# Encoder trunk on one core: up-projection loads that alternate between two buffer tags, and the last plain pair reordered

## The chip, the cores and the metric

One core of a Trainium2 chip runs the whole program. The time is the device time of one execution in microseconds (us), as the median of the runs shown. All data is float32; each matmul operand is held as a high and a low part, and three matmuls (high x high, high x low, low x high) make one product step.

## The reference

Two layers on x of 1024 rows x 1024 columns. Layer 0 has a gated spatial mixer, layer 1 a banded attention; the change touches neither. Each is followed by the same feed-forward block (FFN), which is where the change lies:

```python
def sq_relu_mlp(h, w_up, w_down):
    return jnp.square(jax.nn.relu(h @ w_up)) @ w_down

h = h + rms_norm(m, g[1])
f = sq_relu_mlp(rms_norm(h, g[2]), w_up[layer], w_down[layer])
h = h + rms_norm(f, g[3])
```

`w_up` is 1024 x 4096 and `w_down` 4096 x 1024.

## The kernel before

**FFN up stage.** `ffn` (L380 on) computes relu(z w_up)^2, with z the normed stream. It goes through 16 pairs j of 128-column strips of `w_up`: strip j and strip j + 16. With z cut into four blocks (z11, z12, z21, z22: row halves by column halves) and a pair into b11, b21, b12, b22, a pair is a 2 x 2 block product. Pairs 0 to 2 are "plain": four results, each of two products (`plain`, L518). Pairs 3 to 15 use `blocks` (L555): seven products instead of eight, on sums of the blocks of z (s1, s2, s4, and a third sum that is written over z21 in place by `s3_in_place`, L514) and on differences of the weight blocks. A product is 12 matmuls of 128 x 512 (four steps of three). In `blocks` the products stand in this order on PE: b11 z11, t2 s2, b21 z12, t1 s1, t3 z21, t4 z22, b22 s4. The first and third add up in bank b1, the second and fifth in b2, the fourth and seventh in b3. The seventh may start only when DVE's L596 has read b3.

**Operands.** `load_pair` (L400) loads the two strips of a pair from HBM into two tiles of the tag "raw", which has two buffers. `Prep.step` 0 to 5 (L534) makes the operands out of them: each is a cast to the high part on ACT (L119) and a subtraction for the low part on DVE (L120); in between DVE forms the differences in place (L539, L542, L543, L548). Step 4 makes t3 and step 5 makes t4; after them the raw tiles are free. In `blocks` the steps of the *next* pair stand between the products of the running one, and SP's queue has the loads of pair j + 1 ahead of the spill of pair j - 1 (L464).

**Results.** ACT applies relu and square in place (`squared`, L447), POOL makes five sums of result blocks (`sums`, L452: place 0, then 5 and 6, then 2 and 3), and SP writes seven blocks per pair to `r_dram` (`spill`). `finish` (L610), called one block later, adds the seventh product (L611), squares it and makes sums 2 and 3.

**Order.** Inside the up stage all engines keep the order of the program text (`manual_schedule(engines=ALL)`), each engine in its own queue. The tag "row" has two buffers as well: during the up stage it holds the temporary sums of z, last the two parts of the third sum (`parts`, L512), which `s3_in_place` reads; afterwards `Post` (L290) takes one buffer for the norm weights (loaded by POOL's queue, L112) and one as scratch.

**Block 3 is special before the change** (`first`, L561): it holds the replacement of z21, steps 3 to 5 of its own pair, and, later than in the other blocks, the steps of pair 4:

```python
            nc.scalar.copy(left.t1, b1)
            if first:
                s3_in_place()
                prep.step(3)
                prep.step(4)
            else:
                before.finish()
                step(0)
```

**FFN down stage.** For each of seven products p (L727 on) eight steps jj load a block of `r_dram` (xr, L633) and one or two blocks of `w_down` (xw, L637), split them on ACT and DVE, and run 4 x 6 matmuls. The spill of pair 15 (`before.spill()`) stands at p = 0, jj = 1 of this loop; here a scheduler sets the order on each engine.

Of the kernel before, what the change touches and what calls it, by code (L numbers as in the profile page):

```python
# [18 lines left out]
NT = T // P  # L19
# [42 lines left out]
def trunk_kernel(ctx: ExitStack, tc: tile.TileContext, io: dict):  # L62
    nc = tc.nc
# [13 lines left out]
    ph = Pools(tc)  # L77
# [90 lines left out]
    def load_h(tag, t, h_src):  # L168
        h = ph.t(tag, f"h{t}")
        nc.sync.dma_start(h, h_src)  # L170
        return h
# [55 lines left out]
    def tick():  # L227
        if late:
            late.pop(0)()

    def out_mm(ps, src, units, t, ks):
        cs = slice(t * P, (t + 1) * P)
        for k in ks:
            uH, uL = units[k // 2]
            o = slice((k % 2) * 512, (k % 2) * 512 + 512)
            aH, aL = src(k, cs)
            mm3(ps, aH, aL, uH[:, o], uL[:, o], k == 0, k == NK - 1)
# [24 lines left out]
    def proj_second(src, zn, w, g_post, g_next, m_src, h_src, h_dst, htag, mtags, rest=None):  # L262


        def first(g, m, ps):
            nc.scalar.copy(m[:, 512:], ps[:, :512])
            if rest is not None:
                nc.vector.tensor_add(m[:, :512], ps[:, 512:], m[:, :512])

        tail = Tail(zn, g_post, g_next, h_dst, first)  # L270
        units = [load_unit(w[1, kp], f"wo1{kp}", W4[kp]) for kp in range(4)]
        if rest is not None:
            raw = ph.t("raw", "wo03r")
            nc.sync.dma_start(raw[:, :512], w[0, 3][:, 512:])
            split(rest[:, 0], rest[:, 1], raw[:, :512])
        for t in range(NT):
            ps = ph.t("big", f"po1{t}")
            m = ph.t(mtags[t % len(mtags)], f"m{t}")
            nc.sync.dma_start(m[:, :512], m_src[t])
            h = load_h(htag, t, h_src(t))  # L280
            out_mm(ps[:, :512], src, units, t, range(NK))
            if rest is not None:
                aH, aL = src(NK - 1, slice(t * P, (t + 1) * P))
                mm3(ps[:, 512:], aH, aL, rest[:, 0], rest[:, 1], True, True)
            if t == NT - 1:
                yield
            tail.step(t, (m, ps, h))
        late.extend([lambda i=i: tail.step(NT + i) for i in range(3)])
# [93 lines left out]
    NS = 3  # L382

    def ffn(layer, z, quad, g_post, h_src, h_dst, zn, wtags, utag, rtags):
# [15 lines left out]
        def load_pair(j):  # L400
            r = []
            for c in (j, j + NJ):
                raw = ph.t("raw", f"up{c}r")
                nc.sync.dma_start(raw, wup[c])
                r += [raw[:, o] for o in half]
            return r
# [15 lines left out]

        class Left:


            def __init__(self, j):
                self.j = j
# [86 lines left out]
        def s3_in_place():  # L514
            for i, x in enumerate(parts):
                split(*[q[:, :, 256 * i:256 * i + 256] for q in z21], x)

        def plain(w, left, th, fh):  # L518
            ps = ph.t("ps", f"pu{left.j}{th}{fh}")
            product(ps, w[fh], (z21 if th else z11), last=False)  # L520
            product(ps, w[2 + fh], (z22 if th else z12), first=False)
            return lambda: left.squared(th, fh, ps)

        class Prep:


            def __init__(self, j):
                self.j, self.w = j, {}
                self.b11, self.b21, self.b12, self.b22 = load_pair(j)
# [25 lines left out]
        def blocks(prep, nxt, before):  # L555

            w, left = prep.w, Left(prep.j)
            j = prep.j
            b1, b2 = ph.t("ps", f"pu{j}1"), ph.t("ps", f"pu{j}2")

            first = before.j < NS  # L561

            def step(*steps):
                if nxt is not None:
                    for i in steps:
                        nxt.step(i)

            v = nc.vector.tensor_tensor
            part = dict(skip_group_check=True)
            product(b1, w["b11"], z11, **part)  # L570
            nc.scalar.copy(left.t1, b1)
            if first:
                s3_in_place()
                prep.step(3)
                prep.step(4)
            else:
                before.finish()
                step(0)
            product(b2, w["t2"], s2, **part)
            v(left.u[:, 0], left.t1, b2, op=OP.add)  # L580
            if first:
                prep.step(5)
            else:
                step(1)
            product(b1, w["b21"], z12, first=False, **part)
            left.squared(0, 0, b1)
            step(*(0, 1) if first else (2,))
            b3 = ph.t("ps", f"pu{j}3")
            product(b3, w["t1"], s1, **part)
            step(2 if first else 3)  # L590
            if first:
                before.sums(0, 5, 6, 2, 3)
            before.spill()
            product(b2, w["t3"], z21, first=False, **part)
            v(left.u[:, 1], left.t1, b2, op=OP.add)
            v(left.at(1), left.u[:, 1], b3, op=OP.add)  # L596
            if nxt is None:
                ahead.append(operands(0, 0))
            left.squared(1, 1)
            left.sums(0)  # L600
            step(3 if first else 4)
            b4 = ph.t("ps", f"pu{j}4")
            product(b4, w["t4"], z22)
            v(left.u[:, 1], left.u[:, 1], b4, op=OP.subtract)
            left.squared(1, 0)
            left.sums(5, 6)
            step(*(4, 5) if first else (5,))
            product(b3, w["b22"], s4, first=False, **part)

            def finish():  # L610
                v(left.u[:, 0], left.u[:, 0], b3, op=OP.add)  # L611
                left.squared(0, 1)
                left.sums(2, 3)

            left.finish = finish
            return left
# [35 lines left out]
        with tc.manual_schedule(engines=ALL):  # L652
            work = sums_of_z()

            def some(n):
                for _ in range(n):
                    work.pop(0)()

            left = [Left(0)]
            done = plain(w0, left[0], 0, 0)  # L660
            tick()
            done()
            w1 = plain_operands(load_pair(1), own[1])
            src2 = load_pair(2)
            done = plain(w0, left[0], 0, 1)
            tick()
            done()
            some(1)
            left.append(Left(1))
            done = plain(w1, left[1], 0, 0)  # L670
            tick()
            done()
            assert not late
            some(2)
            plain(w1, left[1], 0, 1)()
            some(1)
            plain(w0, left[0], 1, 0)()
            some(2)
            plain(w0, left[0], 1, 1)()
            left[0].sums(0, 5, 6, 2, 3, eng=nc.vector)  # L680
            w2 = plain_operands(src2, own[0])
            left.append(Left(2))
            prep = Prep(3)
            left[0].spill()
            some(1)
            plain(w1, left[1], 1, 0)()
            some(2)
            plain(w1, left[1], 1, 1)()
            left[1].sums(0, 5, 6, 2, 3, eng=nc.vector)
            left[1].spill()  # L690
            some(1)
            prep.step(0)
            plain(w2, left[2], 0, 0)()
            prep.step(1)
            plain(w2, left[2], 1, 0)()
            prep.step(2)
            plain(w2, left[2], 0, 1)()
            plain(w2, left[2], 1, 1)()
            before = left[2]
            for j in range(NS, NJ):  # L700
                nxt = Prep(j + 1) if j + 1 < NJ else None
                before = blocks(prep, nxt, before)
                prep = nxt
            before.finish()
# [23 lines left out]
        for p, (_, _, _, outs) in enumerate(PRODUCTS):  # L728
            ps = [ph.t("ps", f"pd{p}{tt}") for tt in range(4)]
            final = p == len(PRODUCTS) - 1  # L730
            n = NJ // 2 - (lead if final else 0)
            for jj in range(n):
                rw = ahead.pop() if ahead else operands(p, jj)
                if p == 0 and jj == 1:
                    before.spill()
                for tt in range(4):
                    mms(ps, tt, jj, rw)
                if p >= 5:
                    post.step(jj - 1 + NJ // 2 * (p - 5), range(4))
            if not final:  # L740
                for tt in range(4):
                    evacuate(ps, tt, outs)
# [552 lines left out]
```

## Time and profile before

| | |
|---|---|
| median of 3 runs | 2248.07 us (2244.12 to 2249.76) |
| profiled execution | 2244.61 us, span 2242.8 us |
| granted TensorE clock, mean | 0.987 |
| PE busy | 2133.7 us (95%), 9848 matmuls |
| DVE busy | 1510.0 us (67%) |
| ACT busy | 1049.1 us (47%) |
| POOL busy | 598.2 us (27%) |
| largest wait of PE | for DVE's L596, 24 times, 43.8 us |

PE's busy share is that of overlapping matmuls: a 128 x 512 matmul is shown with 0.39 us, while the next one starts 0.23 us after it. So lost time is read from the distance of starts, and from the idle time that a row shows in brackets with the instruction that ended it. The stretches meant here are the up stages, 378 to 658 us in layer 0 and 1639 to 1922 us in layer 1 from block 3 on.

### The profile page before, as it was taken

To read this page: it belongs to the slowest core of one execution; us is meant where nothing else is said; L and a number is where in the kernel's file an instruction comes from. 1 tells how busy PE (TensorE), PEld (TensorE's weight loads), DVE (VectorE), ACT (ScalarE), POOL (GpSimd) and SP (SyncE) were. 2 spreads that over 40 slices of the span, in tenths; PEclk is the share of its full clock that TensorE was granted. 3 is DMA by queue.
4 is the path that set the end of the run, shared out by engine and by line. 5 is a ranking of instruction groups with operands and counts; after the bars stand their busy time and mean duration, and the time that the engine had idled before them with its cause. 6 is when DMAs were issued, how large, how long until landed. Compare 5 with 4: busy or idle time off the path is not lost. (4 is left out here: it accounts for less than half of the span.)

```text
span 2242.8 us, 26750 instructions
## 1 busy us (share of the span) xinstructions
PE 2133.7 (95%) x9848; PEld 1748.3 (78%) x9848; DVE 1510.0 (67%) x2214; ACT 1049.1 (47%) x1755; POOL 598.2 (27%) x395
## 2 busy tenths in 40 slices
PE   8999999899999999989999999999989999999997
PEld 6888777677778888868888878777867777888886
DVE  6745287666647677757887877856956666586477
ACT  5333254444445344545565556654534444443342
POOL 1000011233333453461111111101023333364333
PEclk9999999999999999989999999999999999999999
DMA  4122342443458887741111111144343443896775
GB/s 169 53 70 70 135 143 102 146 153 117 143 203 300 285 294 264 268 147 40 50 50 41 50 50 50 57 163 154 125 134 116 145 142 126 292 326 257 273 267 216
DMA packets 113508, 347.01 MB, mean 155 GB/s; under 512 B 11360, under 2 KB 11360, under 8 KB 113376
## 3 DMA queue, kind: packets, MB, share of 16 engines
q1 hardware_dynamic: 112224, 341.11, 43.7%
q0 software_dynamic: 1152, 4.19, 0.6%
q8 instruction: 77, 1.26, 0.2%
q14 instruction: 55, 0.45, 0.1%
HBM read 261.89 MB, written 83.36 MB: 154 GB/s over the span
## 5 line engine op out<-in xcount | busy, mean ns | idle before, releaser
L639 POOL TENSOR_TENSOR xw<-xw,xw 128x1024 f32<-128x1024 f32 x80 | 218.1, 2727 | 274.3 <-DMA xw<-in_w_dn 247.5
L139 PE MATMUL pu<-z,wt 128*128 128x512 f32 x608 | 239.2, 393 | 2.4 <-ACT po L151 2.3
L141 PE MATMUL pu<-z,wt 128*128 128x512 f32 x608 | 237.3, 390 | 0.9 <-DVE wt L120 0.9
L140 PE MATMUL pu<-z,wt 128*128 128x512 f32 x608 | 238.0, 391 | 0.0
L140 PE MATMUL pd<-hlx 128*128 128x512 f32 x448 | 177.3, 396 | 6.3 <-DVE hlx L120 6.3
L139 PE MATMUL pd<-hlx 128*128 128x512 f32 x448 | 176.0, 393 | 4.9 <-ACT hlx L119 4.9
L141 PE MATMUL pd<-hlx 128*128 128x512 f32 x448 | 176.2, 393 | 0.0
L140 PE MATMUL pd<-dn,r 128*128 128x512 f32 x448 | 174.9, 390 | 0.3 <-DVE dn L120 0.3
L139 PE MATMUL pd<-dn,r 128*128 128x512 f32 x448 | 175.0, 391 | 0.0
L141 PE MATMUL pd<-dn,r 128*128 128x512 f32 x448 | 174.8, 390 | 0.0
L139 PE MATMUL pu<-s,wt 128*128 128x512 f32 x312 | 128.6, 412 | 43.8 <-DVE rx L596 24.7
L139 PEld LDWEIGHTS pu<-z,wt 128*128 128x128 f32 x608 | 114.9, 189 | 28.1 <-ACT po L151 2.6
L141 PEld LDWEIGHTS pu<-z,wt 128*128 128x128 f32 x608 | 114.6, 189 | 25.8 <-DVE wt L120 1.3
L140 PEld LDWEIGHTS pu<-z,wt 128*128 128x128 f32 x608 | 114.8, 189 | 23.8
L141 PE MATMUL pu<-s,wt 128*128 128x512 f32 x312 | 126.0, 404 | 3.6 <-DVE wt L120 3.6
L120 DVE TENSOR_TENSOR hlx<-xr,hlx 128x1024 fp32r<-128x1024 f32 x56 | 91.5, 1634 | 51.5 <-ACT hlx L119 51.3
L140 PE MATMUL pu<-s,wt 128*128 128x512 f32 x312 | 125.8, 403 | 0.0
L120 DVE TENSOR_TENSOR r<-xr,r 128x1024 fp32r<-128x1024 f32 x56 | 95.1, 1697 | 45.5 <-ACT r L119 45.4
L120 DVE TENSOR_TENSOR dn<-xw,dn 128x1024 fp32r<-128x1024 f32 x56 | 89.4, 1596 | 42.6 <-ACT dn L119 42.1
L1020 ACT ACTIVATE p<-p,mn 128x640 f32<-128x640 f32 (+4 forms) x128 | 89.2, 697 | 61.1 <-DVE mn L1015 60.3
L120 DVE TENSOR_TENSOR hlx<-xw,hlx 128x1024 fp32r<-128x1024 f32 x56 | 89.0, 1589 | 35.6 <-ACT hlx L119 35.4
L139 PEld LDWEIGHTS pu<-s,wt 128*128 128x128 f32 x312 | 60.5, 194 | 66.6 <-DVE rx L596 29.8
(499 smaller groups left out, 5546.1 us busy)
## 6 DMA issues: line engine op xcount, KB each, us to landing
xw<-in_w_dn SPq DMA_DIRECT2D x192, 512.0 KB, 5.0
xr<-r SPq DMA_DIRECT2D x112, 512.0 KB, 4.9
r<-rx SPq DMA_DIRECT2D x48, 512.0 KB, 3.8
r<-r SPq DMA_DIRECT2D x48, 512.0 KB, 3.8
h<-h SPq DMA_DIRECT2D x24, 512.0 KB, 5.2
h<-in_x SPq DMA_DIRECT2D x16, 512.0 KB, 3.5
h<-m SPq DMA_DIRECT2D x16, 512.0 KB, 2.8
braw<-in_rel SPq DMA_DIRECT2D x16, 320.0 KB, 4.5
```

The costliest lines, as they stand in the source:

```text
L120: (eng_l or nc.vector).tensor_sub(dstL, src, dstH.bitcast(F32))
L139: nc.tensor.matmul(ps, aH, bH, start=first, stop=False, **kw)
L140: nc.tensor.matmul(ps, aH, bL, start=False, stop=False, **kw)
L141: nc.tensor.matmul(ps, aL, bH, start=False, stop=last, **kw)
L639: nc.gpsimd.tensor_tensor(ws[0], ws[0], ws[1], op=op)
L1020: nc.scalar.activation(pt[:, :w], pt[:, :w], AF.Exp, bias=mn, scale=-1.0, accum_out=sm)
```

## The change

Six edits:

1. `load_pair` takes the tag "row" instead of "raw" for pairs 4, 6, 8, 10, 12 and 14, so that neighbouring pairs lie in different buffers.
2. The products of pair 2 run in the order (1,0), (0,0), (1,1), (0,1) instead of (0,0), (1,0), (0,1), (1,1); steps 4 and 3 of pair 3, `s3_in_place` and step 5 move between and behind them.
3. `blocks` loses its special case for block 3: it takes the steps of the next pair where the others do, and keeps the sums of pair 2 where they were.
4. Pair 15's spill moves from jj = 1 to jj = 2 of the down loop.
5. In layer 0's projection a tile "turn" is taken from the PSUM tag "big" ahead of the last tile's matmuls, and one column of it is set to zero ahead of them and behind them.
6. The load of the post-norm weights, which needs a "row" tile, comes later on POOL's queue as a consequence of 1.

```diff
@@ proj_second
             h = load_h(htag, t, h_src(t))
+            turn = None
+            if t == NT - 1 and rest is None:
+                turn = ph.t("big", "turn")[:, 0:1]
+                nc.vector.memset(turn, 0.0)
             out_mm(ps[:, :512], src, units, t, range(NK))
+            if turn is not None:
+                nc.vector.memset(turn, 0.0)
@@ load_pair
-                raw = ph.t("raw", f"up{c}r")
+                raw = ph.t("row" if j > NS and j % 2 == 0 else "raw", f"up{c}r")
@@ blocks
-            if first:
-                s3_in_place()
-                prep.step(3)
-                prep.step(4)
-            else:
+            if before.finish is not None:
                 before.finish()
-                step(0)
+            step(0)
             product(b2, w["t2"], s2, **part)
             v(left.u[:, 0], left.t1, b2, op=OP.add)
-            if first:
-                prep.step(5)
-            else:
-                step(1)
+            step(1)
...
-            step(*(0, 1) if first else (2,))
+            step(2)
...
-            step(2 if first else 3)
-            if first:
+            step(3)
+            if before.finish is None:
                 before.sums(0, 5, 6, 2, 3)
             before.spill()
...
@@ plain pair 2
             prep.step(0)
+            plain(w2, left[2], 1, 0)()
+            prep.step(1)
             plain(w2, left[2], 0, 0)()
-            prep.step(1)
-            plain(w2, left[2], 1, 0)()
             prep.step(2)
+            prep.step(4)
+            prep.step(3)
+            done = plain(w2, left[2], 1, 1)
+            s3_in_place()
+            done()
             plain(w2, left[2], 0, 1)()
-            plain(w2, left[2], 1, 1)()
+            prep.step(5)
@@ down loop
-                if p == 0 and jj == 1:
+                if p == 0 and jj == 2:
                     before.spill()
```

On DVE, in layer 0 around the replacement of z21 (z: that block; up3r and up19r: the two strips of pair 3, up4r and up20r of pair 4; wt: low parts of operands). Before:

```order
L120 TENSOR_TENSOR wt_2358<-up3r,wt_2358 128x512
L120 TENSOR_TENSOR z_169<-zs_2742,z_169 128x4x256
L120 TENSOR_TENSOR z_169<-zs_2782,z_169 128x4x256
L548 TENSOR_TENSOR up3r<-up19r,up3r 128x512
L120 TENSOR_TENSOR wt_2359<-up3r,wt_2359 128x512
L120 TENSOR_TENSOR wt_2357<-up19r,wt_2357 128x512
L580 TENSOR_TENSOR u_2909<-rx,pu_2911 128x512
L120 TENSOR_TENSOR wt_2358<-up3r,wt_2358 128x512
L120 TENSOR_TENSOR wt_2357<-up4r,wt_2357 128x512
L539 TENSOR_TENSOR up4r<-up20r,up4r 128x512
```

and now (line numbers of the changed file, nine higher in this part):

```order
L120 TENSOR_TENSOR wt_2361<-up3r,wt_2361 128x512
L120 TENSOR_TENSOR wt_2360<-up19r,wt_2360 128x512
L557 TENSOR_TENSOR up3r<-up19r,up3r 128x512
L120 TENSOR_TENSOR wt_2362<-up3r,wt_2362 128x512
L120 TENSOR_TENSOR z_169<-zs_2745,z_169 128x4x256
L120 TENSOR_TENSOR z_169<-zs_2785,z_169 128x4x256
L120 TENSOR_TENSOR wt_2361<-up3r,wt_2361 128x512
L120 TENSOR_TENSOR wt_2360<-up4r,wt_2360 128x512
L548 TENSOR_TENSOR up4r<-up20r,up4r 128x512
L583 TENSOR_TENSOR u_2923<-rx,pu_2925 128x512
```

The two z operations now stand behind steps 4 and 3 of pair 3 and ahead of step 5; the first work on pair 4 (its row, and L539, now L548) stands ahead of the block's own L580 (now L583), as in every later block.

On SP, in layer 0 at the start of the down stage (xr: blocks of results, xw: weights, r from rx: pair 15's spill). Before:

```order
L637 DMA xw_4711<-in_w_dn 128x1024
L637 DMA xw_4961<-in_w_dn 128x1024
L464 DMA r_2352<-rx 128x2x512
L633 DMA xr_4747<-r_2347 128x1024
L464 DMA r_2352<-rx 128x2x512
L464 DMA r_2352<-rx 128x512
L464 DMA r_2352<-rx 128x2x512
L637 DMA xw_4749<-in_w_dn 128x1024
```

and now:

```order
L637 DMA xw_4714<-in_w_dn 128x1024
L637 DMA xw_4964<-in_w_dn 128x1024
L633 DMA xr_4746<-r_2350 128x1024
L637 DMA xw_4748<-in_w_dn 128x1024
L473 DMA r_2355<-rx 128x2x512 x3
L473 DMA r_2355<-rx 128x512
L633 DMA xr_4783<-r_2351 128x1024
L637 DMA xw_4785<-in_w_dn 128x1024
```

Both loads of step jj = 2 now stand ahead of the spill, and those of jj = 3 directly behind it. On POOL the load of the post-norm weights (L112) moves from block 3 to between the first and the second sum of pair 13, where it waits for the low part of t3 of pair 14 (the last reader of a row tile).

## Rows read from the trace of the kernel before

**Rows 1.** PE's waits: engine, line, releaser, us in all, times, longest
```profile
PE pu L139 <- DVE rx L596: 24.7, 12, 7.0
PE pu L139 <- DVE r L596: 19.1, 12, 1.9
```

**Rows 2.** Windows, blocks 3 to 15, both layers: stretch, us, busy by engine
```profile
378.04:657.85 279.81, 257.30 (x1092) 205.87 (x1091) 167.46 (x203) 120.98 (x205) 95.69 (x66) 0.99 0.43 142
1639.01:1922.46 283.45, 258.53 (x1093) 208.36 (x1092) 169.38 (x205) 122.55 (x208) 95.70 (x67) 0.97 0.41 140
```

**Rows 3.** PE's timeline, layer 0: start, us, engine, operation, [idle before, releaser]
```profile
308.27 0.50 PE L139 MATMUL pu<-z,wt 128*128 128x512 f32 x1 [2.34 <-ACT po L151]
...
357.64 0.39 PE L139 MATMUL pu<-z,wt 128*128 128x512 f32 x1
...
378.04 0.39 PE L139 MATMUL pu<-z,wt 128*128 128x512 f32 x1
...
402.39 0.79 PE L139 MATMUL pu<-s,wt 128*128 128x512 f32 x1 [5.28 <-DVE rx L596]
...
425.11 0.50 PE L139 MATMUL pu<-s,wt 128*128 128x512 f32 x1 [0.41 <-DVE r L596]
...
635.92 0.50 PE L139 MATMUL pu<-s,wt 128*128 128x512 f32 x1 [1.54 <-DVE r L596]
```

**Rows 4.** DVE's timeline, layer 0, before and in block 3
```profile
373.07 0.69 DVE L120 TENSOR_TENSOR wt<-up3r,wt 128x512 fp32r<-128x512 f32 x1 [0.98 <-ACT wt L119]
382.52 4.18 DVE L120 TENSOR_TENSOR z<-zs,z 128x1024 fp32r<-128x1024 f32 x2 [8.75 <-ACT z L119]
...
396.42 0.69 DVE L539 TENSOR_TENSOR up4r<-up20r,up4r 128x512 f32<-128x512 f32 x1 [0.82 <-DMA up20r<-in_w_up]
```

**Rows 5.** DVE's timeline, layer 0, end of block 3 and block 13
```profile
409.34 1.77 DVE L120 TENSOR_TENSOR wt<-up4r,wt 128x512 fp32r<-128x512 f32 x1
...
605.24 1.21 DVE L539 TENSOR_TENSOR up14r<-up30r,up14r 128x512 f32<-128x512 f32 x1 [0.49 <-DMA up30r<-in_w_up]
...
614.04 0.69 DVE L596 TENSOR_TENSOR rx<-u,pu 128x512 f32<-128x512 f32 x1
```

**Rows 6.** POOL's timeline, layer 0, blocks 3 and 13
```profile
383.34 2.27 POOL L458 TENSOR_TENSOR r<-r,u 128x512 f32<-128x512 f32 x1
...
407.57 3.00 POOL L458 TENSOR_TENSOR rx<-u,rx 128x512 f32<-128x512 f32 x2 [2.55 <-ACT u L450]
...
604.16 1.74 POOL L458 TENSOR_TENSOR r<-u,r 128x512 f32<-128x512 f32 x1
```

**Rows 7.** SP's DMA issues, layer 0, pair 14's second load
```profile
600.93 0.33 SPq L404 DMA_DIRECT2D up30r<-in_w_up  x1
```

**Rows 8.** ACT's timeline, layer 0, block 3
```profile
380.96 0.59 ACT L571 COPY rx<-pu 128x512 f32<-128x512 f32 x1 [1.46 <-PE pu L141]
```

**Rows 9.** PE's timeline, layer 1
```profile
1639.01 0.39 PE L139 MATMUL pu<-z,wt 128*128 128x512 f32 x1
...
1687.52 0.50 PE L139 MATMUL pu<-s,wt 128*128 128x512 f32 x1 [1.95 <-DVE r L596]
...
1898.93 0.50 PE L139 MATMUL pu<-s,wt 128*128 128x512 f32 x1 [1.80 <-DVE r L596]
```

**Rows 10.** SP's DMA issues, layer 0, start of the down stage
```profile
667.50 0.42 SPq L637 DMA_DIRECT2D xw<-in_w_dn  x1
668.01 0.78 SPq L633 DMA_DIRECT2D xr<-r  x1
```

**Rows 11.** PE's timeline, layer 0, start of the down stage
```profile
673.17 0.73 PE L139 MATMUL pd<-hlx 128*128 128x512 f32 x2 [3.45 <-ACT hlx L119]
674.43 0.79 PE L140 MATMUL pd<-hlx 128*128 128x512 f32 x1 [0.52 <-DVE hlx L120]
...
677.92 0.40 PE L140 MATMUL pd<-hlx 128*128 128x512 f32 x1
```

**Rows 12.** DVE's timeline, layer 0, start of the down stage
```profile
675.90 1.22 DVE L120 TENSOR_TENSOR hlx<-xw,hlx 128x1024 fp32r<-128x1024 f32 x1
```

More of the change, by code (lines that the diff above doesn't have):

```diff
@@ L423, in ffn @@
         class Left:
+            finish = None
             def __init__(self, j):
@@ L559, in blocks @@
             b1, b2 = ph.t("ps", f"pu{j}1"), ph.t("ps", f"pu{j}2")
-            first = before.j < NS
             def step(*steps):
@@ L600, in blocks @@
             left.sums(0)
-            step(3 if first else 4)
+            step(4)
             b4 = ph.t("ps", f"pu{j}4")
@@ L606, in blocks @@
             left.sums(5, 6)
-            step(*(4, 5) if first else (5,))
+            step(5)
             product(b3, w["b22"], s4, first=False, **part)
```

## Prediction

> **What bounds the kernel now.** I read the waits of PE first, then PE's timeline in the two FFN up stages, then DVE, POOL, ACT and SP beside it. PE is busy for 95% of the span, so time can come only from the places where its matmuls stand further apart than they must. From 357.64 to 378.04, the start of block 3 of layer 0, 90 matmuls follow each other at 20.40/90 = 0.2267 us [rows 3]; a product (12 matmuls) is 2.72 us, a block (84) 19.04 us. The largest wait of PE is for L596, 24 times, 43.8 us in all [rows 1]: the seventh product of a block, which adds to the PSUM bank that L596 reads. Blocks 3 to 15 take 279.81 us in layer 0 and 283.45 us in layer 1 [rows 2], where 13 blocks at PE's pace would be 247.5: some 32 and 36 us over. Two things make this up. Block 3 is far behind: its seventh product starts at 402.39, not at 378.04 + 72 x 0.2267 = 394.4, and that of block 4 at 425.11. After that a block takes (635.92 - 425.11)/10 = 21.08 us [rows 3], in layer 1 (1898.93 - 1687.52)/10 = 21.14 us [rows 9].
>
> **Block 3.** DVE reaches the replacement of z's third block only at 382.52, in the middle of block 3, and needs 4.18 us for it beside POOL's sums; steps 3 to 5 of pair 3 stand behind it. So the raw tiles of pair 3 come free late, pair 4 lands late, and DVE starts on its second load at 396.42 after waiting for the DMA [rows 4]. The change moves all of this ahead of block 3. The same number of products runs before block 3, so its first product still starts at 378.04.
>
> Its new course: DVE is done with step 2 of pair 3 at 373.76; three more operations of 0.69 us give 375.8, and the two z operations, twice as large, 2.8 us more (up to 4.2 as in [rows 4]): 378.6. Then the second row tile is free, and pair 4's second load takes 4.3 us from issue to DVE's start on it, as in block 13 (600.93 to 605.24) [rows 5, 7]: 382.9. The copy after the first product stands at 380.96 [rows 8]; its 0.6, a cast of 0.6 and a low part of 1.4 beside POOL give 383.5, which is after the load. From there L539 to the end of L596 takes 614.73 - 605.24 = 9.5 us in block 13 [rows 5]: 393.0. But here POOL has five sums of pair 2 to do, so about two more DVE operations take 1.77 instead of 0.69 us [rows 5]: 395.1. PE's own pace asks for 394.4, so it waits 0.7 us there. Bounds: no further contention (393.0, and PE sets the time), or four such operations (397.2).
>
> **From block 4 on I expect no gain**, which decides the size. The load of the next pair will now be there half a block early, since its buffers were freed a block before and SP comes to it behind the spill of the pair before. What goes is the 0.49 us that DVE waits before L539 [rows 5]. But L539 runs while POOL makes its last two sums, and ends 0.55 us after them (606.45 against 605.90) [rows 5, 6]. Where DVE went straight on to its next operation beside two sums of POOL, at 409.34, that operation took 1.77 us and again ended 0.54 us after POOL (411.11 against 410.57) [rows 5, 6]. So an L539 that starts 0.5 us earlier ends at the same time. Everything else in the loop, DVE and ACT handing squares, casts and low parts to each other, takes no load. It is longer than PE's 19.04 us and stays at 21.08.
>
> The Trainium skill (SBUF - State Buffer, Who interferes with whom) has the rule for this: a VectorE operation with two SBUF inputs and a reading GpSimd operation exclude each other for a whole instruction, and the later one blocks. By that rule too the earlier load buys nothing here, and the sum is the same; it speaks against this part of the change. The two pairs of rows agree with it (0.55 and 0.54 us).
>
> Hence the chain of block 4 ends one period after that of block 3. Layer 0: 395.1 + 21.08 = 416.2 against 425.11, a gain of **8.9 us** (6.8 to 10.9). Layer 1, with the same offset of 17.1 us from the start of block 3 at 1639.01 [rows 9]: 1656.1 + 21.14 = 1677.2 against 1687.52, **10.3 us** (8.2 to 12.3). All later blocks and stages move up by this.
>
> **The down stage.** Pair 15's spill moves behind the loads of jj = 2. In layer 0 the weight of jj = 2 was issued at 667.50, behind the spill [rows 10], and PE waited 3.45 and 0.52 us and then took 3.49 us for 8 matmul steps instead of 1.81 [rows 11] (512 columns in 0.43 us, the lower of its two levels, 1.2 GHz): 5.6 us. Now both loads of jj = 2 stand ahead of the spill. Next late is jj = 3: its first load moves one place, from 668.01 to 667.50, so its weight's low part, 675.90 to 677.12 [rows 12], comes 0.5 us earlier, at 676.6, and PE wants it about 5.44 us after 669.4, that is at 675. So 1.5 to 2.5 us stay; gain **3.0 us** (0 to 5.6). Layer 1 had no such wait; 0.
>
> **At nothing:** the two memsets of "turn" (128x1, on DVE): the order puts both together ahead of the last projection tile, and the first up product waits, as before, for ACT alone; between a loss of 0.1 and a gain of 2.3 us, the whole wait there [rows 3]. I take 0, since the releaser stays ACT. POOL's load of the post-norm row moves from block 3 to between the first two sums of pair 13. It waits there for step 4 of pair 14 on DVE, which is done before the square that POOL's next sum waits for, so 0. Without that cover two sums would be late by its issue; they are not in the loop of DVE and ACT, but the spill is behind them on SP, which has half a block to spare.
>
> **Sum:** 8.9 + 10.3 + 3.0 = 22.2 us (14 to 31). The profiled execution took 2244.61 us (span 2242.8), 3.5 below the median 2248.07 of the runs; taken from the median, 2225.9.
>
> **Rivals.**
> - *A, the load was the cause of the whole wait.* Then blocks run at PE's pace: the seventh product of block 4 at 378.04 + 156 x 0.2267 = 413.4 and 1674.4, gains of 11.7 and 13.1; ten blocks each save 2.04 and 2.10, 41.4; with the 3.0 it is 69 us: 2179. For it: 24 equal waits, and a DMA wait in each block. Against it: that wait is 0.49 us of some 2. Chance 0.05. The Trainium skill (Trainium Kernel Development and Optimization, Best Practices) tells to double-buffer so that transfers overlap compute; the expectation behind such a rule is this case.
> - *B, L539 does start and end earlier*, keeping its 1.21 us: 0.49 x 22 = 10.8 us more, 2215. Against it is the pair of rows at 409.34. Chance 0.15.
> - *C, the chain is late in block 3 for another reason* (pair 4 landing late, squares waiting behind the casts of z on ACT). It needs some 9 us in each layer to eat the gain; then 2241 to 2248. Chance 0.10.
> - *D, slower.* The contention turns against POOL: with its loads present DVE never pauses, and POOL's last two sums take 2.27 each, as at 383.34, instead of 3.00 together [rows 6]; L539 ends behind them, so the loop grows by 1.5 us: 22 x 1.5 = 33, and 2225.9 + 33 = 2259. It decides from 22.2/22 = 1.0 us a block. Against it: at 407.57 two sums beside back-to-back DVE work took 3.00, as in block 13. Chance 0.04.
>
> **How the numbers follow.** The forecast has 0.66; its bounds, 2217 to 2234, with the spread of runs (2244.1 to 2249.8) give 2213 to 2235 of its own. The range 2210 to 2236 takes in B and leaves out A, C and D, 0.19. A measurement of this kernel tells about 0.3%, 6.7 us, from no change: faster is the forecast, A and B, 0.86; same is C, 0.10; slower D, 0.04.
>
> **What would show it.** Right: the z operations on DVE ahead of block 3; no wait of 2 or 5 us in block 3; seventh products of blocks 4 to 14 still 21.0 to 21.1 us apart, with PE waiting 1.4 to 1.9 us for L596, and no DMA of an up pair as releaser; L539 taking about 1.77 us; the 3.45 us wait at the start of the down stage gone. Wrong: a period below 20.7 us or PE waits under 1 us (A or B), a seventh product of block 3 over 22 us after its first (C), or sums of POOL over 2 us (D).

## The result, and the profile after

The changed kernel takes **2225.72 us** (median of six runs, 2223.44 to 2230.65), the kernel before 2246.32 us (six, 2244.02 to 2251.15). The ratio is 0.9909 (95% interval 0.9892 to 0.9926): 20.6 us less, against 22.2 forecast from 2248.07 to 2225.9. The profiled execution is the longest of the six (2230.65, span 2228.9), so below single places are compared and not spans. How far a span moves by itself: from the first product of layer 0's down stage to the first of layer 1's up stage it takes 1561.53 - 647.58 = 913.95 us here, 1568.05 - 658.08 = 909.97 before, and 904.8 to 914.3 in the experiments, with nothing different in the program there but the place of one spill, of one load on POOL's queue, and POOL's last sums.

PE's waits in the changed kernel (engine, line, releaser, us in all, times, longest):

```profile
PE pu L139 <- DVE r L596: 18.1, 12, 1.8
PE pu L139 <- DVE rx L596: 12.5, 10, 1.7
```

43.8 us in 24 waits [rows 1] have become 30.6 in 22. The two long ones of block 3, 5.3 and 7.0 us, are gone; those of the later blocks stand nearly as they were (31.5 us then).

Windows from block 3 to the end of the up stage, both layers (columns as in [rows 2]):

```profile
377.89:647.35 269.46, 254.02 (x1092) 204.04 (x1091) 167.49 (x198) 116.93 (x202) 94.45 (x66) 1.00 0.42 148
1632.50:1902.11 269.61, 254.26 (x1093) 206.19 (x1092) 166.79 (x199) 116.18 (x201) 95.22 (x66) 0.99 0.41 146
```

Against 279.81 and 283.45 [rows 2] this is 10.4 us less in layer 0 and 13.8 in layer 1. Where in the stage, PE's timeline shows: the seventh products of blocks 3, 4 and 14 of layer 0, and of blocks 4 and 14 of layer 1:

```profile
394.48 0.39 PE L139 MATMUL pu<-s,wt 128*128 128x512 f32 x1
...
414.56 0.50 PE L139 MATMUL pu<-s,wt 128*128 128x512 f32 x1 [0.61 <-DVE r L596]
...
625.42 0.50 PE L139 MATMUL pu<-s,wt 128*128 128x512 f32 x1 [1.55 <-DVE r L596]
...
1668.81 0.50 PE L139 MATMUL pu<-s,wt 128*128 128x512 f32 x1 [0.79 <-DVE r L596]
...
1879.88 0.50 PE L139 MATMUL pu<-s,wt 128*128 128x512 f32 x1 [1.82 <-DVE r L596]
```

Block 4's stands 10.55 us earlier than the 425.11 of [rows 3]. From there the period is (625.42 - 414.56)/10 = 21.09 and (1879.88 - 1668.81)/10 = 21.11 us, where it was 21.08 and 21.14. All of the gain is in the first two blocks, and 1.6 us in the last one of layer 1 (from block 14's seventh product to block 15's it is 19.2 us, where it was 20.8).

**The granted clock** has a part in both. Two windows of the kernel before: from block 3's seventh product in layer 0, which PE began after a wait of 5.28 us, and from block 14's seventh product to block 15's in layer 1:

```profile
402.39:408.10 5.71, 5.71 (x13) 4.46 (x14) 2.58 (x4) 3.61 (x7) 1.80 (x2) 0.50 0.00 0
1898.93:1919.74 20.81, 20.81 (x84) 17.01 (x85) 6.99 (x8) 8.23 (x13) 6.80 (x5) 0.92 0.46 167
```

and the same places in the changed kernel:

```profile
394.48:400.20 5.72, 5.72 (x27) 4.74 (x26) 2.87 (x3) 2.80 (x6) 2.66 (x3) 1.00 0.24 92
1879.88:1899.09 19.21, 19.21 (x84) 15.87 (x85) 6.12 (x7) 6.61 (x11) 6.83 (x5) 1.00 0.42 147
```

The seventh number, after the five engines' busy times, is the granted clock. At 0.50, which is 1.2 of 2.4 GHz, 13 matmuls started in 5.7 us, where 27 start now. The 1.6 us of layer 1's last block are about what a clock of 0.92 takes from 20.81 us (1.7). Block 4's seventh product stood 22.72 and 23.18 us behind block 3's, more than a period, and stands 20.08 and 19.99 us behind it now. How much of that is the clock's, no run separates.

DVE in block 3 of layer 0:

```profile
375.34 2.35 DVE L120 TENSOR_TENSOR z<-zs,z 128x1024 fp32r<-128x1024 f32 x2
...
383.64 1.67 DVE L548 TENSOR_TENSOR up4r<-up20r,up4r 128x512 f32<-128x512 f32 x1
...
392.89 0.69 DVE L596 TENSOR_TENSOR rx<-u,pu 128x512 f32<-128x512 f32 x1
...
404.56 1.66 DVE L548 TENSOR_TENSOR up5r<-up21r,up5r 128x512 f32<-128x512 f32 x1
```

The z operations stand ahead of the block and take 2.35 us instead of 4.18 [rows 4]; L596 ends at 393.58, before PE asks for it. In the last row pair 5's load has long landed, and L548 (L539 before) follows the low part ahead of it without a pause. It still ends only at 406.22, 0.55 us behind POOL's sum:

```profile
403.94 1.73 POOL L467 TENSOR_TENSOR rx<-u,rx 128x512 f32<-128x512 f32 x1
```

**Start of the down stage.** The wait for step jj = 2 is gone, and another of nearly the same size is there for jj = 3. PE, and the granted clock just behind:

```profile
666.76 0.49 PE L139 MATMUL pd<-hlx 128*128 128x512 f32 x1 [2.36 <-ACT hlx L119]
...
668.12 0.79 PE L140 MATMUL pd<-hlx 128*128 128x512 f32 x1 [0.86 <-DVE hlx L120]
```

```profile
667.00:672.00 5.00, 4.13 (x10) 3.10 (x10) 3.83 (x4) 3.14 (x3) 0.00 (x0) 0.54 0.83 274
672.00:680.00 8.00, 8.00 (x32) 6.45 (x32) 5.78 (x5) 4.61 (x5) 0.00 (x0) 0.86 0.87 291
```

I add up over the first 32 us of the stage how much further apart than 0.2267 us the matmuls start: 6.7 us before, 7.0 us now in layer 0, and 0.0 before, 2.4 us now in layer 1. So the spill's new place gained nothing. The waits are shorter, but the granted clock behind them is 0.54 over five us and 0.86 over the next eight, a mixture of its two levels; before, it was 0.66 from 673 to 678 and 1.00 from there on.

### The profile page after: what moved, and what is told of

Same layout as the page of the kernel before. It is cut to its first block, busy times and chain, and to the rows that moved or that the text cites. A ratio compares the mean times of both kernels' runs of the same rounds, so it can differ in the third digit from the quotient of the medians.

```text
span 2228.9 us, 26792 instructions
## 1 busy us (share of the span) xinstructions
PE 2131.2 (96%) x9848; PEld 1744.4 (78%) x9848; DVE 1508.5 (68%) x2216; ACT 1046.1 (47%) x1755; POOL 607.1 (27%) x395
## 5 line engine op out<-in xcount | busy, mean ns | idle before, releaser
L139 PE MATMUL pu<-s,wt 128*128 128x512 f32 x312 | 126.0, 404 | 30.7 <-DVE r L596 18.1
L141 PE MATMUL pu<-s,wt 128*128 128x512 f32 x312 | 123.7, 396 | 0.0
L140 PE MATMUL pu<-s,wt 128*128 128x512 f32 x312 | 123.7, 396 | 0.0
L120 DVE TENSOR_TENSOR r<-xr,r 128x1024 fp32r<-128x1024 f32 x56 | 88.7, 1584 | 45.1 <-ACT r L119 44.9
L119 ACT CAST tH<-ptr 128x512 fp32r<-128x512 f32 x192 | 80.9, 421 | 68.9 <-PE ptr L1043 67.0
```

What stands on the lines that cost most here:

```text
L119: nc.scalar.copy(dstH, src)
L120: (eng_l or nc.vector).tensor_sub(dstL, src, dstH.bitcast(F32))
L139: nc.tensor.matmul(ps, aH, bH, start=first, stop=False, **kw)
L140: nc.tensor.matmul(ps, aH, bL, start=False, stop=False, **kw)
L141: nc.tensor.matmul(ps, aL, bH, start=False, stop=last, **kw)
```

## The experiments

Each kernel is the changed one with a further edit, unless said. Ratios are to the kernel before, measured on the same chip; they are taken over the runs and can differ by 0.002 from the quotient of the medians. "Offset" is from the second product of block 3 to the seventh of block 4, so what happens in block 3; "period" is from the seventh product of block 4 to that of block 14, over ten. Both are given for layer 0 / layer 1.

| kernel | median us | ratio (95%) | offset us | period us |
|---|---|---|---|---|
| before | 2246 to 2249 | 1 | 44.35 / 45.79 | 21.08 / 21.14 |
| changed | 2225.72 | 0.9909 (0.9892 to 0.9926) | 33.95 / 33.59 | 21.09 / 21.11 |
| alternation alone | 2231.95 | 0.9942 (0.9921 to 0.9963) | 39.30 / 39.28 | 21.09 / 21.10 |
| reordering alone | 2227.08 | 0.9909 (0.9892 to 0.9927) | 34.23 / 34.77 | 21.08 / 21.09 |
| spill back, no turn | 2222.17 | 0.9880 (0.9864 to 0.9896) | 33.96 / 33.59 | 21.09 / 21.11 |
| a sum made twice | 2235.00 | 0.9945 (0.9926 to 0.9964) | 34.47 / 34.06 | 21.53 / 21.51 |
| no late sums | 2176.54 | 0.9693 (0.9672 to 0.9714) | 33.18 / 32.64 | 19.31 / 19.33 |
| spill behind jj = 3's loads | 2224.40 | 0.9894 (0.9877 to 0.9911) | 33.97 / 33.57 | 21.09 / 21.11 |
| casts first | 2208.74 | 0.9822 (0.9807 to 0.9836) | 34.13 / 33.93 | 20.44 / 20.49 |
| both of the last two | 2208.15 | 0.9820 (0.9805 to 0.9835) | 34.14 / 33.93 | 20.44 / 20.47 |
| casts earlier | 2180.89 | 0.9688 (0.9665 to 0.9711) | 33.17 / 32.64 | 19.31 / 19.04 |
| casts earlier, all raw | 2178.40 | 0.9695 (0.9673 to 0.9716) | 33.17 / 32.64 | 19.31 / 19.04 |

### Which half of the change gains

The alternation alone, in the kernel before:

```diff
-                raw = ph.t("raw", f"up{c}r")
+                raw = ph.t("row" if j > NS and j % 2 == 0 else "raw", f"up{c}r")
```

> The kernel before with the alternation of the loads between raw and row tiles alone; everything else stays. Theory (the load ends no wait that counts): the seventh products of blocks 4 to 14 stay 21.0 to 21.2 us apart and PE keeps waiting 1.4 to 1.9 us for L596 in each; in block 3 pair 4's load is now released by the reads of the third sum, some us before step 5 of pair 3, so up to 0.8 us earlier per layer: 2246 us, from 2244 to 2248. Rival A (the load is the whole wait): blocks at PE's 19.04 us, some 40 us less, 2205. Rival B (L539 starts and ends 0.49 us earlier): 10.8 us less, 2235.

Measured 2231.95. The period is what the theory said, the time is not: it missed by 14 us. The offsets fell by 5.1 and 6.5 us, 11.6 together. SP's queue shows how. In this kernel:

```profile
384.94 0.34 SPq L404 DMA_DIRECT2D up4r<-in_w_up  x1
387.18 0.33 SPq L404 DMA_DIRECT2D up20r<-in_w_up  x1
```

and in the kernel before:

```profile
389.60 0.34 SPq L404 DMA_DIRECT2D up4r<-in_w_up  x1
390.80 0.33 SPq L404 DMA_DIRECT2D up20r<-in_w_up  x1
```

The row tiles come free by the z operations in the middle of block 3, the raw tiles only by steps 3 to 5 behind them. The loads go out 3.6 to 4.7 us earlier in layer 0 and 4.7 to 5.7 in layer 1, and block 3's seventh product comes 3.9 and 4.9 us sooner after its second. The rest of the 11.6 us lies between the seventh products of blocks 3 and 4 (21.57 and 21.56 us apart, 22.72 and 23.18 before), where the clock was low in the kernel before. I had put it at 0.8 us, the one DMA wait that DVE's rows show at 396.42 [rows 4]. But the wait ahead of it, for ACT's cast of up4r, was a wait for the load as well: ACT in the kernel before:

```profile
394.26 0.62 ACT L119 CAST wt<-up4r 128x512 fp32r<-128x512 f32 x1 [4.07 <-DMA up4r<-in_w_up]
```

The reordering alone (raw tiles for all, spill at jj = 1, no turn):

```diff
-                raw = ph.t("row" if j > NS and j % 2 == 0 else "raw", f"up{c}r")
+                raw = ph.t("raw", f"up{c}r")
-                if p == 0 and jj == 2:
+                if p == 0 and jj == 1:
```

> The changed kernel with all pairs loaded into raw tiles again, the spill of pair 15 at jj = 1 and without turn: what is left is the reordering of pair 2 and block 3. Theory: pair 4's second load is released by step 5 of pair 3, under 1 us later than by the z operations, and still lands before DVE comes to it, so the seventh product of block 4 is again some 10 us earlier than before in both layers and the whole gain of 20.6 us is there: 2226 us, from 2223 to 2231. Rival (the alternation is needed, because pair 4 and the pairs behind it land too late without it): half of the gain or less, 2236 or more, with a DMA wait of DVE of over 2 us in block 3.

Measured 2227.08, the ratio of the whole change. Pair 4's second load is issued at 379.84 behind step 5, and DVE waits 1.30 us for it, but PE is still fed in time. So the two halves are not a sum: both remove the late start on pair 4, and behind the reordering nothing is left for the alternation. Its period of 21.08, with raw tiles, against 21.09 with the alternation is the direct measure of what an earlier load is worth in the later blocks: nothing. The Trainium skill (Trainium Kernel Development and Optimization, Best Practices) tells to double-buffer so that transfers overlap compute; these periods show a case where the transfer was not what set the pace.

### What sets the period

One more sum on POOL, beside and behind L548:

```diff
-                left.sums(2, 3)
+                left.sums(2, 3, 3)
```

> The changed kernel with POOL's last sum of each block (place 3) made twice, right behind each other, so that POOL has one more sum of 1.2 to 1.3 us beside DVE's L548 and the operations behind it. Theory (POOL's sums beside DVE are in the loop that sets the period): the period of blocks 4 to 14 grows from 21.1 to about 22.3 us, PE's waits for L596 from 1.5 to some 2.7 us, and the time by 22 x 1.2 = 26 us to 2252, from 2244 to 2258. Rival (POOL's sums only lie beside the loop, the loop being ACT's squares and casts): period unchanged, 2226.

Measured 2235.0, 9.3 us over the changed kernel; the period grew by 0.44 and 0.40 us. The direction is the theory's, the size a third of it. POOL and DVE in a block of layer 0:

```profile
511.79 3.45 POOL L467 TENSOR_TENSOR r<-u,r 128x512 f32<-128x512 f32 x2
```

```profile
512.42 1.67 DVE L548 TENSOR_TENSOR up10r<-up26r,up10r 128x512 f32<-128x512 f32 x1
514.01 0.68 DVE L583 TENSOR_TENSOR u<-rx,pu 128x512 f32<-128x512 f32 x1
514.61 1.18 DVE L120 TENSOR_TENSOR wt<-up26r,wt 128x512 fp32r<-128x512 f32 x1
```

L548 is as long as it was. The extra sum runs mostly beside L583, one of whose inputs is in PSUM and which keeps its 0.68 us; only the low part behind it is stretched, from 0.68 to 1.18, and ends 0.55 us after POOL (515.79 against 515.24). The Trainium skill (SBUF — State Buffer, Who interferes with whom) says that a VectorE instruction with at most one SBUF input, outside the modes that use both port pairs, doesn't contend with GpSimd; the 0.68 us of L583 agree.

The opposite: the kernel leaves out the sums of places 2 and 3 in pairs 3 to 15 and fills their places with zeros.

```diff
+                    if i in (2, 3) and self.j >= NS:
+                        nc.gpsimd.memset(self.at(i), 0.0)
+                    else:
-                    eng.tensor_tensor(self.at(i), p, q, op=op)
+                        eng.tensor_tensor(self.at(i), p, q, op=op)
```

> The changed kernel with POOL's sums of places 2 and 3 left out in pairs 3 to 15: a fill with zeros, which reads nothing, stands in their place, so the two seventh parts of the result are zeros. Theory: the low part ahead of L548 takes 0.7 instead of 1.4 us and L548 0.7 instead of 1.7, and as both stand in the loop the period falls by 1.4 to 1.7 us, to about 19.5 (19.04 is PE's own), PE's waits for L596 to under 0.6 us; 22 blocks give some 33 us: 2193, from 2182 to 2205. Rival (the loop doesn't pass through them): period 21.1, 2226.

Measured 2176.54, 49 us less, and 22 blocks at 21.1 - 19.3 us make 39 of them. DVE's low part and its difference (now L551) without POOL beside them:

```profile
519.17 0.69 DVE L120 TENSOR_TENSOR wt<-up11r,wt 128x512 fp32r<-128x512 f32 x1 [1.87 <-ACT wt L119]
519.89 0.69 DVE L551 TENSOR_TENSOR up11r<-up27r,up11r 128x512 f32<-128x512 f32 x1
```

In the changed kernel, with the sums beside them:

```profile
508.51 1.37 DVE L120 TENSOR_TENSOR wt<-up10r,wt 128x512 fp32r<-128x512 f32 x1 [1.87 <-ACT wt L119]
509.92 1.67 DVE L548 TENSOR_TENSOR up10r<-up26r,up10r 128x512 f32<-128x512 f32 x1
```

That is 1.66 us less. Of PE's waits for L596 (L599 here) the profile lists one, of 0.32 us. With the sums left out, the loss at the start of the down stages, 7.0 and 2.4 us, went to zero in both layers, which is the rest. So POOL's late sums are in the loop. With them out of it PE sets the pace in layer 0; in layer 1 the seventh product still starts some 0.3 us late from block 7 on, so the period stays at 19.33.

### The start of the down stage

> The changed kernel with pair 15's spill at jj = 1 again and without turn. What the prediction said: the spill's move was worth 3.0 us in layer 0 and 0 in layer 1, so 2229 with it undone. What the traces now suggest as theory: in layer 0 PE loses about as much at the start of the down stage with the spill at jj = 1 (6.6 to 7.0 us) as at jj = 2 (7.0), and in layer 1 it loses 0 to 0.6 instead of 2.4; so the time is the same or 2 us lower, 2224, from 2219 to 2229. The first product of the up stage in layer 0 waits 2.3 us for ACT with and without turn.

```diff
-                if p == 0 and jj == 2:
+                if p == 0 and jj == 1:
```

Measured 2222.17 (turn's lines are taken out as well), 3.5 us under the changed kernel; the two intervals just overlap. PE loses 6.7 us in layer 0 and 2.3 in layer 1, as with the spill at jj = 2. So the spill's place is worth nothing that these runs can tell, and the 2.4 us of layer 1 aren't its doing, though I had taken them for that. The reordering alone differs from this kernel only in the tags of the loads, and its PE loses 6.6 and 0.6 us there; the alternation alone loses 7.2 and 0.5. So among these kernels layer 1's loss came only with both halves together; by what way, no run shows. The first up product waits 2.34 us for ACT as before, so turn does nothing.

Why the spill's move gained nothing, the rows of the changed kernel show. POOL's last two sums, and DVE beside them:

```profile
653.77 2.27 POOL L467 TENSOR_TENSOR rx<-rx,u 128x512 f32<-128x512 f32 x1
655.99 2.26 POOL L467 TENSOR_TENSOR rx<-u,rx 128x512 f32<-128x512 f32 x1
```

```profile
652.65 2.23 DVE L120 TENSOR_TENSOR hlx<-xr,hlx 128x1024 fp32r<-128x1024 f32 x1
654.81 2.31 DVE L120 TENSOR_TENSOR hlx<-xw,hlx 128x1024 fp32r<-128x1024 f32 x1
```

and SP:

```profile
649.36 9.80 SPq L473 DMA_DIRECT2D r<-rx  x4
659.25 0.78 SPq L633 DMA_DIRECT2D xr<-r  x1
660.13 0.59 SPq L637 DMA_DIRECT2D xw<-in_w_dn  x1
```

The loads of jj = 2 are now in time, so DVE makes their low parts at once, and does so beside POOL's last sums. Before, these sums were alone but for the end of the last one, and the DVE operation that met it was the one that was lengthened:

```profile
664.48 1.28 POOL L458 TENSOR_TENSOR rx<-rx,u 128x512 f32<-128x512 f32 x1
665.72 1.29 POOL L458 TENSOR_TENSOR rx<-u,rx 128x512 f32<-128x512 f32 x1
```

```profile
666.12 1.97 DVE L120 TENSOR_TENSOR hlx<-xr,hlx 128x1024 fp32r<-128x1024 f32 x1 [2.76 <-ACT hlx L119]
```

Counted from the start of the stage, the sums now end 1.7 us later (10.7 us behind it, 8.9 before), with them the spill, and both loads of jj = 3 stand behind it: the first goes out 659.25 - 647.58 = 11.7 us after the stage began, where it was 668.01 - 658.08 = 9.9 us.

Would the spill behind jj = 3's loads do better?

```diff
-        def operands(p, jj):
+        def operands(p, jj, then=None):
...
+            if then is not None:
+                then()
...
-                rw = ahead.pop() if ahead else operands(p, jj)
-                if p == 0 and jj == 2:
-                    before.spill()
+                rw = ahead.pop() if ahead else operands(p, jj, before.spill if p == 0 and jj == 3 else None)
```

> The changed kernel with pair 15's spill on SP's queue directly behind the loads of jj = 3, ahead of their casts (one of which is written over the tiles that the spill reads). Theory (PE's loss at the start of the down stages is due to loads that stand on SP behind the spill, which waits for POOL's last sum): the loads of jj = 3 are there in time, their cast waits only for the spill to land, so the 7 us lost in layer 0 fall to 0 to 3 and the 2.4 us of layer 1 to 0 or 1: about 6 us less than the changed kernel, 2219, from 2215 to 2224. Rival (the wait moves on by one step once more, to jj = 4 or to the cast of jj = 3): 2226.

Measured 2224.4: no gain, as the rival said. PE loses 5.4 us in either layer. Now the cast of jj = 3 waits for the spill to land, since it is written over the tiles that the spill reads:

```profile
665.51 1.05 ACT L119 CAST hlx<-xr 128x1024 fp32r<-128x1024 f32 x1 [9.53 <-DMA r<-rx]
```

### A shorter loop

If DVE and ACT wait for each other, the order on ACT should matter:

```diff
+            step(4)
             left.squared(1, 1)
             left.sums(0)
-            step(4)
...
+            step(5)
             left.squared(1, 0)
             left.sums(5, 6)
-            step(5)
...
+            step(0)
             if before.finish is not None:
                 before.finish()
-            step(0)
```

> The changed kernel with three steps of the next pair each moved ahead of the pair of squares beside it, so that on ACT the cast of t3, of t4 and of b11 stands ahead of relu and square instead of behind them; the step that was behind finish stands ahead of it. No sum, load or product is changed. Theory (the loop is DVE and ACT handing work to each other: three times in a block DVE idles 1.9 us for a cast that stands behind 1.3 us of squares): the loop loses up to 3 x 1.3 us and falls under PE's own pace, the period becomes 19.0 to 19.6 us, PE waits under 0.3 us for L596; 22 blocks give 33 to 45 us: 2187, from 2178 to 2196. Rival (POOL's late sums alone set the period; the squares and so the sums come later and DVE runs into them elsewhere): period 20.5 or more, 2212 or more.

Measured 2208.74, the best so far but 17 us gained instead of 39, and a period of 20.44 and 20.49 us: between theory and rival. ACT at the start of a block, and DVE behind it:

```profile
523.29 0.59 ACT L578 COPY r<-pu 128x512 f32<-128x512 f32 x1 [2.79 <-PE pu L141]
523.78 0.62 ACT L119 CAST wt<-up11r 128x512 fp32r<-128x512 f32 x1
```

```profile
524.43 0.69 DVE L120 TENSOR_TENSOR wt<-up11r,wt 128x512 fp32r<-128x512 f32 x1 [3.66 <-ACT wt L119]
```

The chain has turned to PE: the cast of b11 is written over what the first product reads, so it waits for the end of that product and then for the copy; DVE stands still for 3.66 us, with L611, which had been ready, queued behind.

> Both together: casts ahead of the squares, and the spill of pair 15 behind the loads of jj = 3. Theory: the two gains add, since one lies in blocks 4 to 14 and the other at the start of the down stage: 6 us under the kernel with the casts first alone, 2181, from 2172 to 2190. Rival (with the later squares the last sums and so the spill come later as well, and the cast of jj = 3 waits for it): no gain over the casts first alone.

Measured 2208.15 with the two edits together: again nothing from the spill's place.

So steps 4 and 5 stay ahead of their squares, `finish` goes ahead of step 0 again, the copy behind that step's cast, and step 2 ahead of the squares beside it (against the changed kernel, without steps 4 and 5):

```diff
-            nc.scalar.copy(left.t1, b1)
             if before.finish is not None:
                 before.finish()
             step(0)
+            nc.scalar.copy(left.t1, b1)
...
+            step(2)
             left.squared(0, 0, b1)
-            step(2)
```

> The changed kernel with the casts of t3, t4 and b21 each ahead of the squares beside them on ACT, the work of finish ahead of step 0 as it was, and the copy of the first product behind the cast of b11. Theory, after the run with the casts first (its loop goes through PE: seventh product, first product, copy, cast of b11, and then DVE to L596): without the copy and L611 in that chain and with the cast of b21 not behind squares the chain loses 0.6 + 0.6 + 0.5 to 1.0 us, so PE's own pace of 19.04 to 19.3 us sets the period and its waits for L596 are gone; 22 blocks at 1.1 us less than 20.45 give 25 us under the kernel with the casts first: 2184, from 2176 to 2193. Rival (POOL's sums 2 and 3 now fall on the low part of b11 and on L548 again and cost as much as is won): period 20.2 or more, 2204 or more.

Measured **2180.89, 3.1% under the kernel before**, as forecast. PE doesn't wait for L596 once. Seventh products of layer 1, blocks 4 and 14:

```profile
1640.97 0.39 PE L139 MATMUL pu<-s,wt 128*128 128x512 f32 x1
...
1831.37 0.39 PE L139 MATMUL pu<-s,wt 128*128 128x512 f32 x1
```

The period in layer 1 is 19.04 us, PE's own; in layer 0 it is 19.31 (see the last section). DVE now waits for PE, at L595:

```profile
527.25 0.69 DVE L595 TENSOR_TENSOR u<-r,pu 128x512 f32<-128x512 f32 x1 [1.65 <-PE pu L141]
```

And the same with every pair in raw tiles:

```diff
-                raw = ph.t("row" if j > NS and j % 2 == 0 else "raw", f"up{c}r")
+                raw = ph.t("raw", f"up{c}r")
```

> The same, but with all pairs loaded into raw tiles, so without the alternation of the loads. Theory (the alternation is worth nothing only as long as the loop of DVE and ACT is the longer one): the raw tiles are freed by step 5 near the end of a block, the loads take 4.3 us from issue, and the cast of b11 and L548 at the start of the next block wait for them 1 to 3 us; the period is 20.0 to 21.5 us, and the time 15 to 45 us over that of the same kernel with the alternation. Rival (the loads are in time without it here too): the same time within 4 us.

Measured 2178.4, the same time: the rival. With the casts earlier the raw tiles come free earlier too. SP and DVE:

```profile
530.88 0.33 SPq L411 DMA_DIRECT2D up28r<-in_w_up  x1
```

```profile
535.51 1.67 DVE L548 TENSOR_TENSOR up12r<-up28r,up12r 128x512 f32<-128x512 f32 x1
```

From issue to L548 it is 4.6 us, and this load lands 4.2 to 4.4 us after its issue: just enough. So even with PE as the bound the alternation buys nothing that these runs can tell.

## Why the prediction was right, and where it was not

- **Block 3: right, undersized.** The chain stood as described; gains of 10.4 and 13.8 us in the windows against 8.9 and 10.3. The step that was off is "about two more DVE operations take 1.77 instead of 0.69 us": the squares of pair 2 now come earlier, POOL starts its sums at 377.07 instead of 379.58, and from L548's start to L596's end DVE takes 393.58 - 383.64 = 9.94 us, 0.4 over block 13's 9.5, not 2.1 over. Rival C is out: the seventh product stands 394.48 - 377.89 = 16.6 us after the first, at PE's own pace. Layer 1 gained 1.9 us more than forecast up to block 4's seventh product, and the 1.6 us of the last block, for which the prediction has no term: there the granted clock was low before.
- **No gain from block 4 on: right, and the rows fit the reason given.** The period didn't move (21.09 and 21.11), with and without the alternation. L548 took 1.66 to 1.67 us (1.77 forecast) and ended 0.55 us behind POOL. That POOL's sums are in the loop was argued then; the kernels without the late sums and with one more show it. Rivals A, B and D are out: no period below 20.7, and no sum of POOL over 2 us in the blocks.
- **The down stage: wrong.** "Gain 3.0 us" measured -0.2 in layer 0 (the loss there, taken as 5.6 us, is 6.7 by the starts of the matmuls). The step that failed is "its first load moves one place ... so its weight's low part comes 0.5 us earlier": that took the spill's end as fixed. Rival D's price, 2.27 us a sum, which I had looked for in the blocks, was paid here. In layer 1, put at 0, 2.4 us were lost; neither place of the spill brings them back. With one half of the change alone it is 0.6 and 0.5 us, and the cause is open.
- **Turn and POOL's late load:** nothing, as said: the wait for ACT is 2.34 us with and without turn, and behind the load (607.80) POOL's next sums start at 609.63, 3.97 us after the first, as in block 10 without a load (3.96).
- **The sum:** 10.4 + 13.8 - 0.2 - 2.4 = 21.6 us by places, 20.6 by medians. That it lies so near 22.2 is partly luck: 5.0 too little in the up stages, 5.6 too much in the down stages.
- **Of the two halves** I took the reordering for the one that gains. That holds for the whole change, but the alternation alone would have brought 14 us, which neither the prediction nor the expectation saw.

## What to carry to other kernels

Ask what an operation's *end* hangs on before paying for an earlier start: a load half a block earlier was worth nothing in the later blocks, since the operation behind it ended with another engine's sum. Where two engines hand work to each other, the order of independent work on the one that is asked (casts ahead of squares) can be worth more than a buffer: 45 us here, against nothing. And two edits that remove the same lateness don't add up; each has to be run alone.

## What was not expected of the hardware

- POOL and DVE lengthen each other at the same time: POOL's sum grew from 1.29 to 2.27 us beside back-to-back low parts on DVE, and those from 1.22 [rows 12] to 2.23 and 2.31. Rival D had the price for POOL, but not this place.
- With the casts earlier nothing in the rows holds PE, yet a block takes 19.31 us in layer 0 and 19.04 in layer 1, with the same instructions and a granted clock of 1.00 in both. In layer 0 some matmuls start 0.234 us apart instead of 0.227. In the changed kernel this is hidden: its waits for L596 are 0.27 us shorter in layer 0 than in layer 1, and the period the same. The cause is open.
